# A hybrid encoder layer on one core: the mixer's gate branches as woven seven-product pairs, with the residual parked in DRAM

## The chip, the core and the metric

The kernel runs on one core of a Trainium2 chip. The core has five engines that work at the same time, each through its own instructions in order: TensorE (PE, matrix products), VectorE (DVE), ScalarE (ACT), GpSimd (POOL) and SyncE (SP), which here only issues transfers. On-chip data lie in SBUF, the results of matrix products in PSUM, here in eight banks of 128 x 512 float32. The metric is the device time of one execution in microseconds, lower being better; the median of several runs is given.

## The reference

One layer on 256 tokens with 2048 channels, all in float32:

```python
x = layer_norm(ALPHA*x + 0.5*swiglu(x, ffn1_w1, ffn1_w3, ffn1_w2), ln1_g, ln1_b)
mix = hybrid_mixer(x, w_in, ...)
x = layer_norm(ALPHA*x + mix, ln2_g, ln2_b)
x = layer_norm(ALPHA*x + 0.5*swiglu(x, ffn2_w1, ffn2_w3, ffn2_w2), ln3_g, ln3_b)
x = x + sigmoid(x @ w_ple_gate) * (p @ w_ple_proj)

# hybrid_mixer(x): IN_COLS = 13,320 columns of w_in
mq, mk, mv, mo, mi, mf, sq, sk, sv, ga, gb = split(x @ w_in)   # ga, gb: 2048 columns each
y_m  = mlstm(conv_silu(mq, mk), mv, mi, mf), normed per head, * sigmoid(mo)   # 4 heads of 256
y_sb = stick_breaking(sq, sk, sv)                                             # 8 heads of 128
merged = sigmoid(ga) * (y_m @ w_up_m) + sigmoid(gb) * (y_sb @ w_up_sb)
return merged @ w_out
```

The two FFNs have 5632 hidden channels. What matters here is `ga` and `gb`: both are products of the same x with two 2048 x 2048 blocks of `w_in`.

## The kernel before

Every product of activations and weights is made to float32 precision from three passes: the weight tile and the activation are each split into a high part (an ACT cast to float32r, L1066 for weights) and a low part (a DVE subtraction, L1070), and PE adds high x high, high x low and low x high (L1117 to L1119). A weight tile is 256 rows by 512 columns, 512 KB, loaded by SP (L1039) into a page called `raw`; its two halves of the split take two pages called `split`. The smallest piece of the program is a `Unit`: one weight tile against one half of the tokens (128 of 256), six matmuls. A plain `group` (L310) makes 512 columns from 8 weight tiles, 16 units in two PSUM banks, and each weight tile is split once for two units.

In the FFNs most pairs of up-projections (w1 and w3 on the same x) run as `seven` (L320): a scheme of Strassen's kind in Winograd's form. x, taken as 2 x 2 blocks (token halves by depth), times the two weight matrices side by side needs seven block products instead of eight. It needs sums of blocks. Sums of activations are made once per chunk (`form_turn`, L285, four DVE additions and two splits) into a second set of transposed activations, `act.forms`. Sums of weights are made in the raw page: an accumulating transfer on POOL's queue adds another quarter from DRAM into a page that has been split and used (`grow`, L334 to L337), or DVE adds two raw pages (`plus`, L339 to L344). The seven products are numbered and run in the order one, five, six, two, four and then seven and three in turn; each operand is split once for one unit. Four PSUM banks are in use in turn: X and E from the common pool, B and W the two fixed banks `seeded`. The order of several such pairs is chained (`chained`, L361), with empty places, and `weave` (L157) spreads this list evenly among the units of plain groups.

The whole order is written out ahead by a planner. It walks the list `program`, emits each unit, and keeps its own clock of PE time (L1120). Work that follows (transposes, heads, norm rows) is spawned with a delay on that clock from the table `DELAY` (L44) and emitted when due; `until` (L86) brings it forward where the next unit needs it. Splits are emitted as soon as fewer than SPLIT_MIX (6 in the mixer) tiles are split and unused, loads as soon as fewer than RAW_MIX (5 in the mixer) raw pages are held (L32, L33, L1020 to L1027, L1032). Each engine then executes its own instructions in exactly that order. SBUF holds 44 pages; PSUM has six banks in a common pool besides the two fixed ones.

The mixer before runs only plain groups, one after the other: the columns of q, the head gates, the other q and k, v, mo, the stick-breaking q, k and v, then the gate branches (`branch`, L908, ga and gb of a column group) and the up-projections (`ups`, L911), then w_out. Heads are spawned beside: `mlstm` (L761) and `stick` (L810), chains of small steps on PE, ACT, DVE and POOL (the masks at L834 and L842 are POOL's). The branches' results go through a sigmoid into pages `gt` (L885); `up_done` (L892) multiplies the up-projections into them. The residual `xres` (two tiles of 128 x 2048) stays in SBUF throughout: norm 1 writes it row by row (`rows`, L455, 16 DVE operations), and it is next read when w_out is added (`out_done`, L925).

Of the kernel before, what the change touches and what calls it, by code (L numbers as in the profile page):

```python
# [31 lines left out]
RAW_FFN, RAW_MIX, RAW_EDGE, RAW_HELD = 16, 5, 4, 8  # L32
SPLIT_FFN, SPLIT_MIX, SPLIT_EDGE, SPLIT_HELD = 5, 6, 11, 8  # L33
# [11 lines left out]
    "gb": 12.0, "form": 14.0, "ln_turn": 3.4, "ln_step": 1.2, "ln_low": 2.6, "h": 8.0, "silu": 6.0, "late": 9.0, "rest": 1.2, "mt": 3.2,  # L45
# [46 lines left out]
class ActT:  # L92


    def __init__(self, alloc, forms=None):
        self.alloc = alloc
# [84 lines left out]
def kernel(  # L181
# [16 lines left out]
    ps_pool = ctx.enter_context(tc.tile_pool(name="ps", bufs=PSUM_BUFS, space=bass.MemoryType.PSUM))  # L198
    seed_pool = ctx.enter_context(tc.tile_pool(name="seed", bufs=1, space=bass.MemoryType.PSUM))
# [12 lines left out]
    def drop(n=1):  # L212
        temps[0] -= n
# [66 lines left out]
    def finished(act, c, t):  # L280
        act.mark(c, t, 4)
        if act.forms and all(act.ready(c, h) for h in range(TT)):
            sched.spawn(form_turn(act, c), DELAY["form"] + 3.0 * c)
# [36 lines left out]
    def seven(wa, wb, rows, col0, cols, act, done):  # L320
# [24 lines left out]
        one, five, six, two, four, rest = [], [], [], [], [], []  # L345
        for i in range(n):
# [34 lines left out]
    class Norm:  # L381
        def __init__(self, g, b, act, alpha, delay, step):
            self.g_in, self.b_in, self.act = g, b, act
# [71 lines left out]
        def rows(self):  # L455
# [14 lines left out]
            pages[0] -= 4  # L470

# [106 lines left out]
    x1T = ActT(act_tile)  # L578
    norm1 = Norm(ln1_g[0], ln1_b[0], x1T, None, 30.0, 6.0)
# [4 lines left out]
    flags = set()  # L584

# [273 lines left out]

    head = group(w_in, range(0, D, 2 * P), 0, COL, x1T, qk_done(0, 0))  # L860
    program.extend(skewed(head[:SKEW]) + flat(head[SKEW:]))
    program.extend(flat(group(w_in, range(0, D, 2 * P), 4096, 2 * HM + 2 * DS, x1T, gates_done)))
    for which, g in ((0, 1), (1, 0), (1, 1)):
        program.extend(flat(group(w_in, range(0, D, 2 * P), which * 1024 + g * COL, COL, x1T, qk_done(which, g))))
    program.append(load_norm_m)
    program.append(lambda: [sched.spawn(in_sequence([mlstm(a), mlstm(a + 1)])) for a in (0, 2)])
    for g in range(2):
        program.extend(flat(group(w_in, range(0, D, 2 * P), 2048 + g * COL, COL, x1T, v_done(g))))
    for g in range(2):
        program.extend(flat(group(w_in, range(0, D, 2 * P), 3072 + g * COL, COL, x1T, mo_done(g))))  # L870
    first = 2
    for n in (4, 4, 4, 4, 4, 2):
        program.extend(flat(group(w_in, range(0, D, 2 * P), sq0 + first * DS, n * DS, x1T,
                                  lambda ps, t, f=first, n=n: sb_columns(ps, t, f, n))))
        first += n
        if first == 18:
            program.append(lambda: [sched.spawn(in_sequence([stick(a), stick(a + 2), stick(a + 4), stick(a + 6)]))
                                    for a in (0, 1)])
# [6 lines left out]
    def gate_done(g, half):  # L885
        def done(ps, t):
# [270 lines left out]
```

## Time and profile before

| | |
|---|---|
| median of 3 runs | 2210.81 us (2210.7 to 2211.28) |
| the profiled execution's own time | 2211.03 us, its span 2209.3 us |
| PE busy | 2194.2 us, 10068 matmuls |
| DVE busy | 1683.9 us |
| ACT busy | 1268.7 us |
| POOL busy | 187.5 us |
| splits of weight tiles on DVE | 1013, 1182.3 us |
| read from and written to DRAM | 497.96 MB, 2.10 MB |

The span runs from the first to the last instruction of the profiled execution. A row of a group names the line, the engine, the operation, the tiles written and read, their shapes and the count, then busy time and the mean of one in ns, then the idle time of the engine before it and what ended that. A row of waits gives the total, the number and the longest. In a row by stretch, each engine has its busy time and its instructions; then come the granted clock of PE, the share of the 16 transfer engines' time, and GB/s. Shares over 1 can occur, as transfers of several queues overlap.

### The profile page before, as it was taken

How to read it: one execution, taken by the hardware profiler on the slowest of the kernel's cores; microseconds unless marked ns; L12 is line 12 of the kernel's file. 1: busy time of each engine (PE TensorE's matmuls, PEld its weight loads, DVE VectorE, ACT ScalarE, POOL GpSimd, SP SyncE). 2: the span in 40 equal slices, each digit the busy share in tenths (PEclk: the TensorE clock that was granted, in tenths of full speed). 3: DMA queues.
4: the chain of work that ended last, by engine and by line, in shares of the span. 5: the costliest groups of instructions: out<-in, count | busy, mean ns of one | idle time of the engine just before them, and what ended most of it. 6: DMA issues, size and time to landing. Idle time of an engine off the chain costs nothing.

```text
span 2209.3 us, 27558 instructions
## 1 busy us (share of the span) xinstructions
PE 2194.2 (99%) x10068; PEld 1820.1 (82%) x10068; DVE 1683.9 (76%) x1859; ACT 1268.7 (57%) x1529; POOL 187.5 (8%) x167
## 2 busy tenths in 40 slices
PE   9999999999999999999999999999999999999999
PEld 7888888888887888888888888888888888888878
DVE  6889998888898784654445456599898989889884
ACT  6556566666575555545643344556666666666562
POOL 3111011110100000000100000011011111110000
PEclk9999999999999999999999999999999999999999
DMA  9899889987992765655566666579879998989643
GB/s 347 220 254 269 247 255 294 271 244 216 279 352 70 219 195 167 183 170 163 162 186 185 191 222 218 203 172 316 254 235 247 302 258 249 247 268 302 216 143 96
DMA packets 263050, 501.89 MB, mean 227 GB/s; under 512 B 15841, under 2 KB 24961, under 8 KB 262913
## 3 DMA queue, kind: packets, MB, share of 16 engines
q1 hardware_dynamic: 228096, 433.00, 59.0%
q0 software_dynamic: 34816, 67.12, 16.9%
q8 instruction: 79, 1.29, 0.2%
q14 instruction: 59, 0.48, 0.1%
HBM read 497.96 MB, written 2.10 MB: 226 GB/s over the span
## 4 chain that ended last, share of the span: by engine, by line
PE 96%; DMA 1%; DVE 1%; ACT 1%; issue 0%; DVEq 0%; ACTq 0%
PE mm L1119 27%; PE mm L1117 27%; PE mm L1118 27%; PE seeded L1117 4%; PE seeded L1119 4%; PE seeded L1118 4%; DMA raw<-in_ffn_w_dram 1%; PE ms L266 1%; DVE split L1070 1%; PE ms L436 0%; ACT split L1066 0%; PE ms L825 0%; PE ms L848 0%; PE ms L776 0%; PE ms L788 0%
## 5 line engine op out<-in xcount | busy, mean ns | idle before, releaser
L1070 DVE TENSOR_TENSOR split<-raw,split 128x1024 fp32r<-128x1024 f32 (+1 forms) x1013 | 1182.3, 1203 | 298.8 <-ACT split L1066 284.5
L1066 ACT CAST split<-raw 128x1024 fp32r<-128x1024 f32 (+1 forms) x1013 | 1018.2, 1037 | 458.0 <-PE mm L1118 123.8
L1117 PE MATMUL mm<-split,actT 128*128 128x512 f32 (+2 forms) x2768 | 1075.9, 389 | 3.1 <-ACT big L973 2.4
L1118 PE MATMUL mm<-split,actT 128*128 128x512 f32 (+2 forms) x2768 | 1064.4, 385 | 4.3 <-DVE split L1070 4.3
L1119 PE MATMUL mm<-split,actT 128*128 128x512 f32 (+2 forms) x2768 | 1065.0, 385 | 2.3 <-DVE actT L271 2.3
L1119 PEld LDWEIGHTS mm<-split,actT 128*128 128x128 f32 x2768 | 520.0, 188 | 107.3 <-DVE actT L271 3.1
L1118 PEld LDWEIGHTS mm<-split,actT 128*128 128x128 f32 x2768 | 520.5, 188 | 105.9 <-DVE split L1070 6.1
L1117 PEld LDWEIGHTS mm<-split,actT 128*128 128x128 f32 x2768 | 520.2, 188 | 104.9 <-ACT big L973 3.3
L336 POOL DMA_DIRECT2D raw<-in_ffn_w_dram x128 | 154.5, 1213 | 1303.5 <-DVE split L1070 646.3
L341 DVE TENSOR_TENSOR raw<-raw 128x1024 f32<-128x1024 f32 x128 | 155.8, 1217 | 11.0 <-DMA raw<-in_ffn_w_dram 11.0
L1117 PE MATMUL seeded<-split,actT 128*128 128x512 f32 x384 | 150.5, 392 | 0.0
L1119 PE MATMUL seeded<-split,actT 128*128 128x512 f32 x384 | 149.5, 389 | 0.0
L1118 PE MATMUL seeded<-split,actT 128*128 128x512 f32 x384 | 149.5, 389 | 0.0
L550 DVE SCALAR_TENSOR_TENSOR xres<-mm,xres 128x512 f32<-128x512 f32 x160 | 108.7, 684 | 22.0 <-PE mm L1119 22.0
L1119 PEld LDWEIGHTS seeded<-split,actT 128*128 128x128 f32 x384 | 72.1, 188 | 15.1
L1118 PEld LDWEIGHTS seeded<-split,actT 128*128 128x128 f32 x384 | 72.1, 188 | 14.7
L1117 PEld LDWEIGHTS seeded<-split,actT 128*128 128x128 f32 x384 | 72.1, 188 | 14.6
L268 ACT CAST actT<-ms 128x512 fp32r<-128x512 f32 x60 | 35.1, 587 | 67.2 <-PE ms L266 65.7
L271 DVE TENSOR_TENSOR actT<-ms,actT 128x512 fp32r<-128x512 f32 x60 | 41.0, 685 | 23.3 <-ACT actT L268 13.3
L238 ACT ACTIVATE temp<-mm 128x512 f32<-128x512 f32 (+1 forms) x38 | 21.8, 575 | 52.5 <-PE mm L1119 52.5
L238 ACT ACTIVATE big<-mm 128x512 f32<-128x512 f32 x20 | 12.0, 598 | 55.8 <-PE mm L1119 55.8
L234 ACT ACT_TABLE_LOAD x29 | 37.2, 1283 | 0.5
(137 smaller groups left out, 663.6 us busy)
## 6 DMA issues: line engine op xcount, KB each, us to landing
raw<-in_ffn_w_dram SPq DMA_DIRECT2D x527, 512.0 KB, 8.1
raw<-in_w_in_dram SPq DMA_DIRECT2D x168, 512.0 KB, 3.7
raw<-in_ffn_w_dram POOLq DMA_DIRECT2D x128, 512.0 KB, 9.5
raw<-in_w_out_dram SPq DMA_DIRECT2D x32, 512.0 KB, 4.7
raw<-in_w_ple_gate_dram SPq DMA_DIRECT2D x24, 512.0 KB, 4.8
raw<-in_w_up_m_dram SPq DMA_DIRECT2D x16, 512.0 KB, 3.9
raw<-in_w_up_sb_dram SPq DMA_DIRECT2D x16, 512.0 KB, 4.1
raw<-in_w_ple_gate_dram SPq DMA_DIRECT2D x16, 256.0 KB, 5.1
```

Of the source, the lines that this page charges most:

```text
L234: nc.scalar.preload_act_table_set(table[0])
L238: nc.scalar.activation(out, in_, func, **kw)
L268: nc.scalar.copy(dst[:, 0], ps[:])
L271: nc.vector.tensor_tensor(out=dst[:, 1], in0=ps[:], in1=dst[:, 0], op=ALU.subtract)
L336: nc.gpsimd.dma_start(out=raw.tile[:, :, :cols], in_=src.src, accum_op=ALU.add)
L341: nc.vector.tensor_tensor(out=a.tile[:, :, :cols], in0=a.tile[:, :, :cols], in1=b.tile[:, :, :cols], op=ALU.add)
L550: nc.vector.scalar_tensor_tensor(out=xs, in0=ps, scalar=0.5, in1=xs, op0=ALU.mult, op1=ALU.add)
L1066: nc.scalar.copy(hi[:, ks], r[:, ks])
L1070: nc.vector.tensor_tensor(out=lo[:, ks], in0=r[:, ks], in1=hi[:, ks], op=ALU.subtract)
L1117: nc.tensor.matmul(ps, hi, w[0][:, k, :u.cols], start=first, stop=False, skip_group_check=u.onto)
L1118: nc.tensor.matmul(ps, hi, w[1][:, k, :u.cols], start=False, stop=False, skip_group_check=u.onto)
L1119: nc.tensor.matmul(ps, lo, w[0][:, k, :u.cols], start=False, stop=last, skip_group_check=u.onto)
```

## The change

The gate branches become `gates7(g)`: for each of the four column groups, ga and gb are made as one seven-product pair from x1T and its sums. The pairs are chained and woven into all plain groups of the mixer from the k columns on, up to the up-projections of the first three groups. For that:

- x1T gets its second set with the sums of blocks (its delay is a new entry, 20).
- `seven` has a second form, `grown`: all sums of weights are made by accumulating transfers, none by DVE. Per depth it loads three quarters plainly and adds four; products three and seven use one buffer one after the other.
- Space: with x1T's sums kept through the mixer, the residual is copied to DRAM (`spill`, on POOL's queue) once norm 1's rows are done, and the gates of the first two column groups are kept in its place; it is read back (`refill`, eight transfers on SP's queue) before w_out. Norm 1's rows start and go faster (16 and 4 for 30 and 6).
- RAW_MIX goes from 5 to 8, SPLIT_MIX from 6 to 4.
- The heads run group by group: k and q of the first half, its v, its two mlstm heads, its mo, then the second half; the stick-breaking columns come in another order, so that the first four heads can start before the columns of the others. The up-projections of the first three groups run first with w_up_m, then with w_up_sb, and wait in the plan for the gates' flags.

```diff
-RAW_FFN, RAW_MIX, RAW_EDGE, RAW_HELD = 16, 5, 4, 8
-SPLIT_FFN, SPLIT_MIX, SPLIT_EDGE, SPLIT_HELD = 5, 6, 11, 8
+RAW_FFN, RAW_MIX, RAW_EDGE, RAW_HELD = 16, 8, 4, 8
+SPLIT_FFN, SPLIT_MIX, SPLIT_EDGE, SPLIT_HELD = 5, 4, 11, 8
...
-            two.append(unit(2, i, Weight(b21, [b21], []), act, 0, 2, "X", False))
-            four.append(unit(4, i, Weight(t, [], [t, b21], plus(t, b21)), act, 1, 2, "E", False))
             b12, b22 = quarter(wb, i, 0), quarter(wb, i, 2)
-            rest.append(unit(7, i, Weight(b12, [b12, b22], [b12], plus(b12, b22)), act.forms, 1, 0, "W", False))
-            rest.append(unit(3, i, Weight(b22, [], [b22]), act.forms, 1, 2, "B", False))
+            if grown:
+                w6.then = grow(t, quarter(wa, i, 2))
+                w2, w4 = Weight(b21, [b21], [b21]), Weight(t, [], [t])
+                w3, w7 = Weight(b22, [b22], []), Weight(b22, [], [b22])
+                w3.then = grow(b22, b12)
...
+        if grown:
+            rest = third[:1] + flat(zip(third[1:], seventh[:-1])) + seventh[-1:]
...
-    x1T = ActT(act_tile)
-    norm1 = Norm(ln1_g[0], ln1_b[0], x1T, None, 30.0, 6.0)
+    x1T = ActT(act_tile, ActT(act_tile), "form1")
+    norm1 = Norm(ln1_g[0], ln1_b[0], x1T, None, 16.0, 4.0, lambda: sched.spawn(spill(), 6.0))
...
+    def spill():
+        for t in range(TT):
+            nc.gpsimd.dma_start(out=kept[t][:], in_=xres[t][:])
+        flags.add("spilt")
...
+    def refill():
+        for c in range(4):
+            for t in range(TT):
+                cs = slice(c * COL, (c + 1) * COL)
+                nc.sync.dma_start(out=xres[t][:, cs], in_=kept[t][:, cs])
+        flags.add("refilled")
...
+    main = columns(1024, COL, qk_done(1, 0))
     for g in range(2):
+        if g:
+            main += columns(COL, COL, qk_done(0, 1)) + columns(1024 + COL, COL, qk_done(1, 1))
+        else:
+            main.append(load_norm_m)
+        main += columns(2048 + g * COL, COL, v_done(g))
+        main.append(lambda g=g: sched.spawn(in_sequence([mlstm(2 * g), mlstm(2 * g + 1)])))
+        main += columns(3072 + g * COL, COL, mo_done(g))
+    for first, n in ((2, 4), (8, 4), (16, 4), (6, 2), (12, 4), (20, 4)):
+        main += columns(sq0 + first * DS, n * DS, lambda ps, t, f=first, n=n: sb_columns(ps, t, f, n))
+        if first == 16:
+            main.append(lambda: [sched.spawn(in_sequence([stick(a), stick(a + 2), stick(a + 4), stick(a + 6)]))
+                                 for a in (0, 1)])
...
+    def gates7(g):
+        def done(m, banks):
+            ps = {k: v["ps"][:] for k, v in banks.items() if v}
+            if m == 5:
+                for t in range(TT):
+                    gt[g, t] = xres[t][:, g * 1024:(g + 1) * 1024] if g < 2 else big()[:]
+                e = temp()
+                nc.scalar.copy(e[:], ps["E"])
+                banks["B"]["ps"], banks["W"]["ps"] = seeded
+                nc.vector.tensor_tensor(out=banks["B"]["ps"][:], in0=ps["X"], in1=e[:], op=ALU.subtract)
+                drop()
+            elif m == 6:
+                nc.scalar.copy(banks["W"]["ps"][:], ps["B"])
+            elif m == 4:
+                nc.scalar.copy(gt[g, 1][:, 0:COL], ps["E"])
+            elif m == 2:
+                sched.spawn(gate(0, 0, ps["X"], 1.0), DELAY["silu"])
+            elif m == 7:
+                c = gt[g, 1][:, 0:COL]
+                nc.vector.tensor_tensor(out=c, in0=ps["W"], in1=c, op=ALU.add)
+                sched.spawn(gate(1, 1, ps["W"], -1.0))
+                sched.spawn(gate(1, 0, c, 1.0), DELAY["silu"])
+            elif m == 3:
+                sched.spawn(gate(0, 1, ps["B"], -1.0))
...
     def up_done(g, half):
         def done(ps, t):
+            sched.until(lambda: ("gate", g, half, t) in flags)
...
-    program.extend(branch(0, 0) + branch(0, 1) + branch(1, 0) + branch(1, 1))
-    program.extend(ups(0) + ups(1))
-    program.extend(branch(2, 0) + branch(2, 1) + ups(2))
-    program.extend(branch(3, 0) + branch(3, 1))
+    for half in range(2):
+        for g in range(3):
+            main += ups(g, half)
+    program.extend(weave(main, chained([gates7(g) for g in range(4)])))
     program.append(lambda: [sched.spawn(merge_turn(g, t), 1.0 + 2.0 * g + t) for g in range(3) for t in range(TT)])
-    program.extend(ups(3))
+    program.append(lambda: sched.spawn(refill(), 14.0))
+    program.extend(ups(3, 0) + ups(3, 1))
```

More of the change, by code (lines that the diff above doesn't have):

```diff
@@ L343, in plus @@
             return make
-        one, five, six, two, four, rest = [], [], [], [], [], []
+        one, five, six, two, four, seventh, third = [], [], [], [], [], [], []
         for i in range(n):
@@ L470, in rows @@
             pages[0] -= 4
+            if self.then:
+                self.then()
     def scaled(xs):
@@ L584 @@
     flags = set()
+    kept = [dram_pool.tile([P, D], F32, name=f"kept{t}") for t in range(TT)]
+    def spill():
+        for t in range(TT):
+            nc.gpsimd.dma_start(out=kept[t][:], in_=xres[t][:])
+        flags.add("spilt")
+        return
+        yield
+    def refill():
[4 more added lines that the diff above has]
+        flags.add("refilled")
+        return
+        yield
     def mixer_setup():
```

66 lines of the change are left out of this document (32 added, 34 removed).

## The prediction

> **What bounds the kernel now.** I read the page's head and its chain of waits first. Its totals by engine, then its chain by engine:
>
> ```profile
> span 2209.3 us, 27558 instructions
> ...
> PE 2194.2 (99%) x10068; PEld 1820.1 (82%) x10068; DVE 1683.9 (76%) x1859; ACT 1268.7 (57%) x1529; POOL 187.5 (8%) x167
> ...
> PE 96%; DMA 1%; DVE 1%; ACT 1%; issue 0%; DVEq 0%; ACTq 0%
> ```
>
> PE is busy for 99% of the span and carries 96% of the chain that ends last, so a matmul taken out is worth its whole time, provided nothing else becomes late. Next, what PE waited for between 690 and 1430 us, which is the mixer with the two norms beside it:
>
> ```profile
> engine line waited for: us in total, times, longest us
> PE mm L1118 <- DVE split L1070: 2.2, 2, 1.1
> ```
>
> Two waits, 2.2 us in all: in the whole mixer PE hardly stops. Third, busy time by stretch: the woven first FFN (100 to 540), two stretches of the mixer's plain groups, and two short stretches where transfers come thickest.
>
> ```profile
> core 0: us, PE busy (x) PEld busy (x) DVE busy (x) ACT busy (x) POOL busy (x), PEclk, DMA share, GB/s
> 100.00:540.00 440.00, 440.00 (x1973) 364.44 (x1972) 389.85 (x384) 271.94 (x290) 57.80 (x48) 1.00 0.90 257
> 730.00:830.00 100.00, 100.00 (x501) 84.33 (x500) 81.16 (x116) 57.43 (x80) 0.00 (x0) 1.00 0.68 205
> 830.00:1000.00 170.00, 170.00 (x774) 139.67 (x773) 92.30 (x142) 84.89 (x110) 8.14 (x8) 1.00 0.58 168
> ...
> 720.00:730.00 10.00, 10.00 (x55) 8.64 (x54) 3.44 (x6) 2.83 (x7) 0.00 (x0) 1.00 0.91 299
> ...
> 1430.00:1440.00 10.00, 10.00 (x45) 8.27 (x45) 6.84 (x10) 5.61 (x8) 0.00 (x0) 1.00 1.04 384
> ```
>
> The FFN already weaves seven-product pairs into plain groups: DVE 389.85 of 440 us (89%), DMA share 0.90, and PE still 440.00 of 440. The mixer has room: DVE 54% to 81%, DMA 0.58 to 0.68. The granted clock is 1.00 throughout.
>
> **The products removed.** The pace of PE, from the first and last matmul of an undisturbed stretch in order of time:
>
> ```profile
> 1139.71 0.39 PE L1119 MATMUL mm<-split,actT 128*128 128x512 f32 x1
> ...
> 1149.91 0.39 PE L1119 MATMUL mm<-split,actT 128*128 128x512 f32 x1
> ```
>
> These are 46 matmuls, so 45 steps in 10.20 us: 0.2267 us each (the 0.39 us shown is a pipelined duration). A unit of the program is six matmuls, 1.360 us. The branches of one column group are now 2 x 8 weight tiles x 2 token halves = 32 units; as a seven-product pair they are 4 depths x 7 = 28. Over four groups 16 units go, 96 matmuls: 96 x 0.2267 = 21.8 us. Everything else on PE (groups, transposes, heads) keeps its count; it is only ordered anew.
>
> **What it adds off PE.** The groups of instructions, different shapes apart:
>
> ```profile
> L1070 DVE TENSOR_TENSOR split<-raw,split 128x1024 fp32r<-128x1024 f32 x979 | 1159.7, 1220 | 282.0 <-ACT split L1066 267.8 <-PE mm L1118 6.0 <-DMA raw<-in_w_in_dram 1.9
> ...
> L1066 ACT CAST split<-raw 128x1024 fp32r<-128x1024 f32 x979 | 999.1, 1052 | 451.2 <-PE mm L1118 123.8 <-PE mm L1119 92.2 <-DVE split L1070 70.6
> ...
> L336 POOL DMA_DIRECT2D raw<-in_ffn_w_dram x128 | 154.5, 1213 | 1303.5 <-DVE split L1070 646.3 <-DMA raw<-in_ffn_w_dram 636.6 <-DVE xres L550 20.0
> ...
> L234 ACT ACT_TABLE_LOAD x29 | 37.2, 1283 | 0.5
> ...
> L504 DVE TENSOR_TENSOR seeded<-mm,temp 128x512 f32<-128x512 f32 x16 | 11.1, 696 | 5.9 <-ACT temp L510 5.9
> ...
> L510 ACT COPY temp<-mm 128x512 f32<-128x512 f32 x16 | 9.4, 585 | 14.2 <-PE mm L1119 14.2
> ...
> L291 DVE TENSOR_TENSOR temp<-temp,big 128x256 f32<-128x256 f32 x8 | 3.7, 462 | 0.3
> ```
>
> A plain weight tile is split once for two units, a seven-product operand once for one: 112 splits where 64 were, 48 more. DVE gets 48 x 1.220 = 58.6 us, the sums of four chunks of x1T at most 4 x (4 x 0.462 + 2 x 0.696) = 13.0, and two ops of 0.69 a group, 5.5: together 77 us. ACT gets 48 x 1.052 = 50.5, eight casts and twelve copies of about 0.6, 12, and up to 24 table loads (each sigmoid batch between exponentials, 31 us): 62 to 93. The woven stretch is 352 full units and 16 of 256 columns (half as many columns, so some 0.7 us, an estimate from the pace above), 352 x 1.360 + 11 = 490 us. There two splits, one plain and one of the pairs, stand in about 4.08 us: 2.44 us of DVE, 60%. The heads' own DVE work is what the 830 stretch holds beside its splits, which alone are:
>
> ```profile
> 830.00:1000.00 170.00, 158.73 (x670) 124.15 (x669) 65.67 (x56) 55.14 (x56) 1.00 0.58 168
> ```
>
> 92.30 - 65.67 = 26.6 us in 170 (third column), 16%. So 76%, below the FFN's 89% at which PE loses nothing: cost 0, hidden under PE. Were that cover gone, the 77 us would count from DVE's first full stretch.
>
> The earlier norm rows (delay 16 for 30) and the sums of x1T fall in the first 60 us of the mixer, where DVE has 81% and gets some 12 us more. That is about full for a while. The lead of the splits absorbs it; I take 0, at most 4.
>
> **Transfers.** FFN first, then the mixer: queues (packets, MB, share of 16 engines), and issues with the median time to landing.
>
> ```profile
> q1 hardware_dynamic: 45477, 87.65, 57.8%
> q0 software_dynamic: 13056, 25.17, 31.7%
> ...
> raw<-in_ffn_w_dram SPq DMA_DIRECT2D x166, 512.0 KB, 7.8
> raw<-in_ffn_w_dram POOLq DMA_DIRECT2D x48, 512.0 KB, 9.5
> ```
>
> ```profile
> q1 hardware_dynamic: 15340, 28.50, 57.5%
> ...
> raw<-in_w_in_dram SPq DMA_DIRECT2D x51, 512.0 KB, 3.6
> ```
>
> The change drops 16 of 64 plain loads of gate weights and adds 64 accumulating ones on POOL's queue, 2.1 MB of the residual out (POOL's queue) and 2.1 MB back (SP's). A plain load takes all 16 engines for 0.578 x 440 / 167 = 1.52 us in the FFN and 0.575 x 170 / 54.4 = 1.80 us in the thin traffic of the mixer; in the thick traffic of the 720 row 9.1 us / 2.99 MB x 0.524 MB = 1.60. An accumulating load takes 0.317 x 440 / 48 = 2.9 us. In the weave: 144 plain loads of w_in, 8 halves, 24 of the up weights, 64 accumulating, and the spill (4 loads' worth). With 1.60 that is 148 x 1.60 + 28 x 1.52 + 64 x 2.9 = 465 us in 490, share 0.95; with 1.52 it is 0.92; with 1.80 and the accumulating loads dearer in the same ratio (3.4) it is 527, more than the stretch. I take 0.95: a little above the FFN's 0.90, and the 1430 row shows that 1.04 and 384 GB/s can be carried.
>
> Is each load early enough? RAW_MIX is 8, but a pair holds up to four first quarters, and in the third/seventh phase (seven side places of 4.08 us, 28 us a group) two sums besides: only 2 to 3 buffers are left for loads, and a load is wanted every 2.8 us (172 loads in 490 us). Sustained, 2.5 buffers allow 2.5 x 2.8 = 7 us from issue to split. A landing of L makes the splits late by 28 x (1 - 7/L) a group, less the lead of the splits (SPLIT_MIX 4: four units stand between, 5.5 us). At the FFN's L = 7.8: 2.9 us, covered. At 10: 8.4 - 5.5 = 2.9 us on PE, 12 over four groups. So 0 to 12; I take 1, since 7.8 is the row with the nearest load.
>
> The accumulated operands:
>
> ```profile
> DMA to landing us min/median/max: 5.9/9.5/14.3
> ```
>
> The shortest gap from a split to the next use of the same buffer is third to seventh: two side places, 8.2 us, plus 5.5 of lead, 13.6 us, at five places (last group's first and last, the others' last with 15.0). Wanted: 2.3 (split) + 9.5 + 2.3 = 14.1. So 0 to 0.5 us each at the median, 5 each at the longest landing: 0 to 25, I take 1.
>
> **Heads, queues, residual.** POOL works in order, and the selects of the heads now stand behind accumulating issues of 1.2 us that wait for their split; who waits for the selects is PE. The selects' own view, then POOL in order of time, then two of PE's steps in the chain:
>
> ```profile
> L834 POOL TENSOR_SCALAR_AFFINE_SELECT temp<-temp x8: 589/729/1389, 1015.4 to 1093.3; 128x256 f32<-128x256 f32 x8
> ```
>
> ```profile
> 1043.27 1.95 POOL L834 TENSOR_SCALAR_AFFINE_SELECT temp<-temp 128x256 f32<-128x256 f32 x2 [17.49 <-DVE temp L833]
> ```
>
> ```profile
> 1047.87 0.65 PE ms L838 x2
> ...
> 1074.05 0.65 PE ms L838 x2
> ```
>
> Between the selects' end (1045.22) and PE's step lie 2.65 us. One issue with its 1.2 us fits; an issue whose split is queued (2.3 us more) makes 0.9 late. Eight such steps: 0 to 7. X and E hold two of six PSUM banks and the main group two, so each pair of stick heads has just two; 12 double steps at one 0.59 us copy: 0 to 7. The last heads start when sv's second half is there (395 us into the weave by the order's unit times) and at 1074.05 - 1047.87 = 26.2 us a pair end just when ups want them (449): 0 to 5. I take 1 for all. The new wait of the up-projections for the gates is on a flag of the plan, and the sigmoids lie many units ahead of it.
>
> The spill is issued some 60 us (by the unit times) before the first gate value is written over the residual, and 2.1 MB at the rates above are 6 us; ACT, with the splits queued behind that gate, would wait only beyond that. The refill is put in SP's queue behind loads and waits for the last transposes of groups 0 and 1; behind it stand the w_out loads. It is issued 7 us before the last up-projections end, and the residual is first read 16 units, 22 us, after that; 6 us of transfer are covered by the eight buffers, which hold only main weights by then. Cost 0; without that cover, 6.
>
> Sum: profiled execution 2211.0 us (span 2209.3 and 1.7 around it, 0.2 above the median of 2210.81): 2211.0 - 21.8 + 1 + 1 + 1 = 2192.
>
> **The rivals.** (1) Short buffers: landings near 10 us, +12 in place of +1: 2203. For: the low-buffer phase and 27% of accumulating transfers, against the FFN's 22%. Against: landings are 3.6 us now, and few requests in flight queue less. (2) Heads late under the weave: selects behind issues and PSUM banks short, +14 in place of +1: 2205. For: POOL has one order, DVE is fuller. Against: heads run in one stream a group now, and a select's longest is 1.39 us. [...]
>
> (3) Transfers of w_in are dearer than I take: halfway from 1.60 to 1.80, with accumulating loads in the same ratio (2.9 x 1.70 / 1.52 = 3.24): 148 x 1.70 + 43 + 64 x 3.24 = 502, 12 over the stretch, 2211.0 - 21.8 + 12 + 2 = 2203. For: 1.80 in the mixer. Against: 1.60 where traffic is thick, as it will be. [...]
>
> (4) The other side: transfers bound the weave. Price: 527 us in 490, +37, so 2211.0 - 21.8 + 37 = 2226. It turns the sign once they pass 490 + 21.8 = 512. For: 1.80, and an accumulating load of w_in has no row, so 3.4 is open. Against: 1.80 with today's accumulate price is only 148 x 1.80 + 43 + 186 = 495, and 1.80 is measured where few loads overlap.
>
> **How the numbers follow.** Forecast 60% (2189 to 2197), (1) 13%, (2) 9%, (3) 8%, (4) 10%. The measurement tells about 0.2%, 4.4 us, from no change: faster is below 2206.4, slower above 2215.2. Forecast and most of (1), (2) and (3) are faster: 83%. Their tails and the start of (4) are the same: 6%. The rest is slower: 11%. The range goes from 2188 (no loss at all is 2189.2) to 2209, past (1) to (3), and leaves out (4).
>
> **What would show it.** PE 96 matmuls fewer (9972) and busy 22 us less; L1070 x1061; POOL's issues of in_w_in x64, landing near 9 us; DMA share about 0.95 in the weave, against 0.58 to 0.68; PE's waits in the mixer below 6 us. Wrong if PE waits for splits whose cast waited for raw transfers (1, 3, 4), or for selects, copies or PSUM (2), or if DVE is at 100% through the weave.

## The result, and the profile after

The changed kernel takes 2228.65 us (median of four runs, 2227.91 to 2231.02), the kernel before beside it 2211.05: a ratio of 1.0081, with an interval of 1.0063 to 1.0098. It is 17.6 us slower, where 18.8 us faster was forecast and the range ended at 2209.

The page's head, three groups and two rows of transfers of the kernel after. A group's row has busy time and mean of one in ns, then idle time before it; a transfer's row has count, size and median time to landing:

```profile
span 2226.7 us, 27777 instructions
...
PE 2187.3 (98%) x9972; PEld 1804.9 (81%) x9972; DVE 1755.1 (79%) x1935; ACT 1332.3 (60%) x1600; POOL 265.5 (12%) x233
...
L1133 DVE TENSOR_TENSOR split<-raw,split 128x1024 fp32r<-128x1024 f32 (+2 forms) x1061 | 1242.4, 1206 | 276.5 <-ACT split L1129 258.9
L1129 ACT CAST split<-raw 128x1024 fp32r<-128x1024 f32 (+2 forms) x1061 | 1065.1, 1038 | 454.2 <-PE mm L1181 112.1
...
L337 POOL DMA_DIRECT2D raw<-in_w_in_dram x64 | 77.2, 1207 | 453.4 <-DVE split L1133 388.2
...
raw<-in_w_in_dram SPq DMA_DIRECT2D x152, 512.0 KB, 4.9
...
raw<-in_w_in_dram POOLq DMA_DIRECT2D x64, 512.0 KB, 7.9
```

The counts are those worked out: 9972 matmuls, 96 fewer; 1061 splits, 48 more; 64 accumulating loads. The other work is near its estimate too: DVE has 71.2 us more (77 were estimated), ACT 63.6 (62 to 93). In this listing the cast of a split is L1129, its subtraction L1133, and the three matmuls are L1180 to L1182. Without 21.8 us of matmuls the span would be 2187.5, so 39.2 us are lost somewhere.

What PE waited for between 690 and 1440 us (total, times, longest):

```profile
PE mm L1181 <- DVE split L1133: 15.9, 17, 2.3
PE mm L1180 <- ACT split L1129: 3.9, 5, 1.4
PE ms L798 <- DVE actT L262: 3.0, 2, 1.8
PE mm L1180 <- DVE big L677: 1.1, 1, 1.1
PE seeded L1180 <- ACT split L1129: 1.0, 1, 1.0
PE seeded L1181 <- DVE split L1133: 0.8, 1, 0.8
PE ms L881 <- DVE actT L262: 0.7, 1, 0.7
PE ms L746 <- ACT temp L734: 0.3, 2, 0.2
```

Where the kernel before had two waits of 2.2 us in all, these are thirty waits of 26.7 us, most of them for a split (L1133 and L1129). Each is short. By stretch (columns: length; busy time of PE, PE's weight loads, DVE, ACT, POOL; granted clock, share of the transfer engines, GB/s), first before, then after:

```profile
730.00:790.00 60.00, 60.00 (x319) 51.18 (x318) 49.36 (x71) 36.56 (x52) 0.00 (x0) 1.00 0.70 209
790.00:1350.00 560.00, 560.00 (x2580) 464.46 (x2579) 306.09 (x385) 280.40 (x363) 18.66 (x24) 1.00 0.61 183
```

```profile
730.00:790.00 60.00, 50.80 (x248) 40.36 (x247) 51.30 (x84) 30.86 (x47) 4.85 (x4) 0.94 0.65 169
790.00:1350.00 560.00, 544.38 (x2478) 445.28 (x2477) 364.83 (x438) 341.30 (x432) 91.90 (x86) 1.00 0.88 234
```

PE is idle for 9.2 us in the first 60 us of the weave and for 15.6 in the rest. DVE is busy for 365 of the 560 us, 65%, and the transfers for 0.88: neither is full on average. Everything ahead of the mixer and behind norm 2 takes as long as before: norm 1's transposes start at 694.5 us (694.1 before), and from norm 2's first transpose to the end of the span it is 809.4 us (809.6 before).

Two places of the kernel after, in order of time (start, duration, instruction, in brackets the idle time before it and what ended it). ACT, then DVE, when the head gates are made:

```profile
745.65 1.04 ACT L1129 CAST split<-raw 128x1024 fp32r<-128x1024 f32 x1
754.59 0.42 ACT L239 ACTIVATE big<-big 4x256 f32<-4x256 f32 x1 [7.90 <-DVE big L704]
755.03 1.28 ACT L235 ACT_TABLE_LOAD   x1
...
757.18 1.98 ACT L1129 CAST split<-raw 128x1024 fp32r<-128x1024 f32 x2
```

```profile
748.41 0.69 DVE L475 TENSOR_TENSOR xres<-xres,big 128x512 f32<-128x512 f32 x1
749.14 0.69 DVE L476 TENSOR_TENSOR xres<-xres,big 128x512 f32<-128x512 f32 x1
749.75 1.29 DVE L262 TENSOR_TENSOR actT<-temp,actT 128x512 fp32r<-128x512 f32 x2
750.95 0.42 DVE L291 TENSOR_TENSOR temp<-big 128x256 f32<-128x256 f32 x1
...
752.42 1.22 DVE L1133 TENSOR_TENSOR split<-raw,split 128x1024 fp32r<-128x1024 f32 x1
...
754.10 0.46 DVE L704 TENSOR_SCALAR big<-ms,bf 4x256 f32<-4x256 f32 x1
758.24 1.23 DVE L1133 TENSOR_TENSOR split<-raw,split 128x1024 fp32r<-128x1024 f32 x1 [3.69 <-ACT split L1129]
```

ACT's next instruction in order is a step of the head gates that needs DVE's L704. DVE comes to it only after norm rows (L475, L476), low parts and sums of x1T (L262, L291 to L294) and a split. ACT stands still for 7.9 us with the casts of the next splits behind that step, and from the end of one cast to the start of the next (746.69 to 757.18) 10.5 us pass; then DVE stands still for 3.7 us, because no cast is ready; then PE waits. The same happens in each convolution, where ACT's scaling of the second half waits for DVE's three additions on the first:

```profile
933.95 0.48 ACT L239 ACTIVATE temp<-ms,cw 128x256 f32<-128x256 f32 x1
936.77 0.47 ACT L239 ACTIVATE temp<-ms,cw 128x256 f32<-128x256 f32 x1 [2.35 <-DVE temp L757]
```

And a wait of PE can have a tail. PE in order of time after its longest wait at the start:

```profile
746.28 0.50 PE L1181 MATMUL mm<-split,actT 128*128 128x512 f32 x1 [2.28 <-DVE split L1133]
746.62 0.39 PE L1182 MATMUL mm<-split,actT 128*128 128x512 f32 x1
...
747.40 0.63 PE L1182 MATMUL mm<-split,actT 128*128 128x512 f32 x1
747.83 0.63 PE L1180 MATMUL mm<-split,actT 128*128 128x512 f32 x1
...
749.97 0.63 PE L1182 MATMUL mm<-split,actT 128*128 128x512 f32 x1
```

One microsecond after the wait, seven matmuls start 0.43 us apart ((749.97 - 747.40) / 6) in place of 0.227, and the granted clock is 0.50 from 747.4 to 750.2 us and 0.94 over the stretch from 730 to 790. There are three such spells in the mixer, 21 matmuls, 4.3 us beyond the waits; most of the thirty waits have none behind them.

So of 39.2 us, 24.5 are new visible waits (26.7 - 2.2) and 4.3 slow matmuls; some 10 are in no row. Part of these are restarts: where no second wait follows, the matmul behind one that waited mostly starts 0.31 to 0.34 us after it (746.28 to 746.62 above) in place of 0.227, for thirty waits some 3 us (an estimate from those rows, 30 x 0.11). By place the visible waits (27.0 us, with a few too short for the rows above) are 9.2 us at the start (730 to 790), 4.9 at the convolutions, 5.1 at the mlstm heads and where a head's step waits for a PSUM bank, 3.8 at the stick-breaking rounds, 1.8 at the last pair's accumulated operand, and 2.2 at the two norms as before.

### The profile page after: what moved, and what is told of

It is laid out like the page before. It is cut to its first block, busy times and chain, and to the rows that moved or that the text cites. A ratio compares the mean times of both kernels' runs of the same rounds, so it can differ in the third digit from the quotient of the medians.

```text
span 2226.7 us, 27777 instructions
## 1 busy us (share of the span) xinstructions
PE 2187.3 (98%) x9972; PEld 1804.9 (81%) x9972; DVE 1755.1 (79%) x1935; ACT 1332.3 (60%) x1600; POOL 265.5 (12%) x233
## 4 chain that ended last, share of the span: by engine, by line
PE 45%; issue 2%; ACT 1%; DMA 1%; DVE 1%; ACTq 0%; POOLq 0%; POOL 0%; DVEq 0%
PE mm L1181 12%; PE mm L1180 12%; PE mm L1182 12%; PE seeded L1181 2%; PE seeded L1182 2%; PE seeded L1180 2%; DMA raw<-in_w_in_dram 1%; PE ms L267 1%; ACT split L1129 0%; ACT temp L239 0%; DVE split L1133 0%; PE ms L449 0%; PE ms L871 0%; PE ms L881 0%; ACT big L1036 0%
## 5 line engine op out<-in xcount | busy, mean ns | idle before, releaser
L1133 DVE TENSOR_TENSOR split<-raw,split 128x1024 fp32r<-128x1024 f32 (+2 forms) x1061 | 1242.4, 1206 | 276.5 <-ACT split L1129 258.9
L1129 ACT CAST split<-raw 128x1024 fp32r<-128x1024 f32 (+2 forms) x1061 | 1065.1, 1038 | 454.2 <-PE mm L1181 112.1
L1181 PE MATMUL mm<-split,actT 128*128 128x512 f32 (+2 forms) x2640 | 1018.0, 386 | 17.8 <-DVE split L1133 17.8
L1180 PE MATMUL mm<-split,actT 128*128 128x512 f32 (+2 forms) x2640 | 1027.7, 389 | 7.7 <-ACT split L1129 4.1
L1182 PE MATMUL mm<-split,actT 128*128 128x512 f32 (+2 forms) x2640 | 1016.7, 385 | 2.3 <-DVE actT L272 2.3
L1181 PEld LDWEIGHTS mm<-split,actT 128*128 128x128 f32 x2640 | 497.3, 188 | 120.0 <-DVE split L1133 25.0
L1180 PEld LDWEIGHTS mm<-split,actT 128*128 128x128 f32 x2640 | 497.1, 188 | 107.4 <-ACT split L1129 8.0
L1182 PEld LDWEIGHTS mm<-split,actT 128*128 128x128 f32 x2640 | 496.8, 188 | 102.1 <-DVE actT L272 3.1
L1180 PE MATMUL seeded<-split,actT 128*128 128x512 f32 x480 | 189.0, 394 | 1.0 <-ACT split L1129 1.0
L1181 PE MATMUL seeded<-split,actT 128*128 128x512 f32 x480 | 187.8, 391 | 0.9 <-DVE split L1133 0.8
L1182 PE MATMUL seeded<-split,actT 128*128 128x512 f32 x480 | 187.5, 391 | 0.0
L337 POOL DMA_DIRECT2D raw<-in_w_in_dram x64 | 77.2, 1207 | 453.4 <-DVE split L1133 388.2
L1181 PEld LDWEIGHTS seeded<-split,actT 128*128 128x128 f32 x480 | 90.4, 188 | 20.3 <-DVE split L1133 2.1
L1180 PEld LDWEIGHTS seeded<-split,actT 128*128 128x128 f32 x480 | 90.3, 188 | 19.9 <-ACT split L1129 1.8
L1182 PEld LDWEIGHTS seeded<-split,actT 128*128 128x128 f32 x480 | 90.4, 188 | 18.9
L239 ACT ACTIVATE temp<-mm 128x512 f32<-128x512 f32 (+1 forms) x38 | 21.8, 575 | 63.7 <-PE mm L1182 63.6
```

Of the source, the lines that this page charges most:

```text
L337: nc.gpsimd.dma_start(out=raw.tile[:, :, :cols], in_=src.src, accum_op=ALU.add)
L1129: nc.scalar.copy(hi[:, ks], r[:, ks])
L1133: nc.vector.tensor_tensor(out=lo[:, ks], in0=r[:, ks], in1=hi[:, ks], op=ALU.subtract)
L1180: nc.tensor.matmul(ps, hi, w[0][:, k, :u.cols], start=first, stop=False, skip_group_check=u.onto)
L1181: nc.tensor.matmul(ps, hi, w[1][:, k, :u.cols], start=False, stop=False, skip_group_check=u.onto)
L1182: nc.tensor.matmul(ps, lo, w[0][:, k, :u.cols], start=False, stop=last, skip_group_check=u.onto)
```

## The theories

**A.** What PE has in hand is the lead of the splits: with n tiles held, n - 1 stand ahead of PE. A plain tile lasts two units, an operand of a pair one; in the weave that is 1.5 units of 1.360 us on average. Before: 5 x 2 x 1.360 = 13.6 us. After, with four: 3 x 1.5 x 1.360 = 6.1 us. ACT and DVE work in order, and the heads, the norm rows and the sums come in bursts in which ACT makes no cast for more than 6 us, at the longest, in the weave, for the 10.5 us above. The old lead covered them, the new one doesn't. Two parts are told apart: **A1**, the work on DVE at the start, and **A2**, ACT standing still in its order for a result of DVE. **B**: the accumulating transfers and the raw buffers are what is late (the prediction's own rivals 1, 3 and 4).

## The experiments

### Transfers or lead

e1: an accumulating load brings only half its bytes.

```diff
-                nc.gpsimd.dma_start(out=raw.tile[:, :, :cols], in_=src.src, accum_op=ALU.add)
+                ks = slice(0, 1 if grown else 2)
+                nc.gpsimd.dma_start(out=raw.tile[:, ks, :cols], in_=src.src[:, ks], accum_op=ALU.add)
```

> Each accumulating transfer of the gate pairs adds only the first of its two 128-row halves, so half the bytes on POOL's queue in the mixer; the second half of the weight sums is left out of the result. Theory A (splits too few ahead, so that bursts of other work on ACT and DVE reach PE): transfers are not what is late, only the last pair's waits for accumulated operands go, 2224 to 2229 us. Rival B (transfers bound the weave, the fourth rival of the prediction): 64 x 1.45 = 93 us of transfers less in the weave, so most of the 39 us lost comes back, 2190 to 2200 us.

Measured: 2224.02 us, ratio 1.0058 (1.0043 to 1.0073). The stretch from 790 to 1350:

```profile
790.00:1350.00 560.00, 546.83 (x2497) 448.88 (x2496) 365.07 (x438) 344.98 (x434) 71.34 (x86) 1.00 0.75 208
```

The transfer share falls from 0.88 to 0.75 and PE gains 2.5 us in 560. What ACT's casts waited for transfers between 725 and 1420, in the changed kernel and then in e1:

```profile
ACT split L1129 <- DMA raw<-in_w_in_dram: 41.6, 14, 7.4
ACT split L1130 <- DMA raw<-in_w_in_dram: 11.1, 9, 4.1
```

Casts that wait for raw transfers are the sign that the prediction named for its rivals 1, 3 and 4, and the changed kernel has them. With e1 three quarters of these waits go, yet PE's waits for splits only fall from 21.6 to 19.4 us. Half the accumulated bytes are worth 4.6 us at most; B isn't the main cause.

e2: one split less, SPLIT_MIX 3 for 4. e4: the kernel before with SPLIT_MIX 3 for 6, a lead of 2 x 2 x 1.360 = 5.4 us, and nothing else.

> The changed kernel with SPLIT_MIX 3 for 4, all else equal. Theory A: one split less ahead of PE (about 4.1 us of lead for 5.5), PE's waits in the mixer rise from 26 us to 40 or more, 2240 to 2260 us. Rival B: the transfers are the same, 2226 to 2231 us.

> The kernel before with SPLIT_MIX 3 for 6 and nothing else: two other weights of two units each stand between a split and its use, 5.4 us of lead, as in the changed kernel, but no pairs, no accumulating transfers, DMA share unchanged near 0.6. Theory A: PE's waits of 10 us or more appear in the mixer at the same kinds of bursts (convolutions, head norms, stick heads), 2220 to 2235 us. Rival B: no change, 2210 to 2212 us.

Measured: e2 2262.9 us, 1.0233 (1.0216 to 1.025); e4 2223.64 us, 1.0056 (1.0041 to 1.0071). PE's waits in the mixer, e2:

```profile
PE mm L1181 <- DVE split L1133: 23.1, 25, 2.1
PE mm L1180 <- ACT split L1129: 12.3, 9, 2.8
```

and e4:

```profile
PE mm L1118 <- DVE split L1070: 7.5, 8, 1.8
PE mm L1117 <- ACT split L1066: 1.8, 3, 1.4
```

e4 is the clearest row of the study. There is no pair, no accumulating load and no sum in that mixer, its transfer share is 0.59 (690 to 1440), and a lead of 5.4 us, a little shorter than the changed kernel's 6.1, costs 12.6 us by itself. e2's time lies 3 us above what was expected; its direction and its waits are A's.

e3: one split more (5), paid with a raw page (RAW_MIX 7), since the pages are all in use.

> The changed kernel with SPLIT_MIX 5 for 4 and RAW_MIX 7 for 8 (a raw page given up for the two split pages, since the pages are full). Theory A: lead 6.8 us for 5.5, PE's waits in the mixer fall by about a third, 2216 to 2224 us. Rival B: one load less in flight in a stretch bound by transfers, 2229 to 2240 us.

Measured: 2229.53 us, 1.008 (1.0065 to 1.0095). The waits for splits fell from 21.6 to 13.7 us, but waits for steps of the heads rose, ACT's waits for transfers went from 41.6 us in 14 to 52.6 in 24, and nothing was gained. Whether the page or the longer lead did that, this run doesn't tell.

### Taking the bursts away

e6 (A2): ACT isn't made to wait in its order. Both scalings of a convolution come ahead of DVE's additions, and the plan lets splits in between a DVE result and the ACT step that reads it.

```diff
                 activate(acc[:, k], ps[:, k], ACT.Copy, scale=w(3))
+            for k in range(2):
+                ...
                 for j in range(3):
...
+        yield 4.0
         activate(sp, zf, ACT.Abs)
...
+        yield 1.3
         activate(st["em"][:], ps[:, 1], ACT.Exp, scale=-1.0)
...
+            yield DELAY["m2"]
             activate(hs[:, t], ps[:, 0:DM], ACT.Copy, scale=r[:, t:t + 1])
```

> The changed kernel with the small steps of the heads put in another order, the work the same: in the convolution both ACT scalings before the DVE additions; one planner step between DVE's result and the ACT step that wants it in the head gates and in mlstm. ACT then waits less for DVE with splits queued behind it. Theory A2 (ACT blocked in order, with 5.5 us of lead): the gaps at the convolutions and mlstm steps (about 6 us with 2 to 4 of tail) go, 2217 to 2224 us. Rival (only the number of splits ahead matters, blocks move elsewhere): 2226 to 2231.

Measured: 2213.78 us, 1.0014 (1.0005 to 1.0023): 14.9 us less than the changed kernel, from the order of a few ACT steps, and more than was expected. ACT's waits for the DVE results concerned (head gates, convolutions, mlstm) fall from 59.6 to 24.2 us. PE's visible waits fall by 6.5 us (26.7 to 20.2), its slow matmuls from 21 to 14; the rest of the gain is in no row. e12, the same edit in the kernel before:

> Control: the kernel before with the same reordering of the heads' small steps and nothing else. Its splits lead PE by about 14 us, so ACT's waits behind DVE are covered: 2210 to 2212 us. If the reordering saves time by itself, below 2208.

2211.71 us, 1.0002 (0.9992 to 1.0011). With a lead of 13.6 us the same ACT stalls cost nothing.

e5 (A1): norm 1's rows move from DVE to POOL, which is busy for 4.85 of the 60 us there.

```diff
-                        nc.vector.tensor_tensor(out=xs, in0=xs, in1=g, op=ALU.mult)
-                        nc.vector.tensor_tensor(out=xs, in0=xs, in1=b, op=ALU.add)
+                        eng = nc.gpsimd if self.then else nc.vector
+                        eng.tensor_tensor(out=xs, in0=xs, in1=g, op=ALU.mult)
+                        eng.tensor_tensor(out=xs, in0=xs, in1=b, op=ALU.add)
```

> The changed kernel with the 16 operations of norm 1's rows on POOL instead of DVE (11 us less on DVE in the first 60 us of the mixer). Theory A1 (part of the loss is DVE being full at the mixer's start, 730 to 790 us: 9 us of PE's 27 us of gaps and two of its three slow spells): about half of these 9 us and of their tail go, 2217 to 2224 us. Rival (the start does not matter, the bursts later do): 2226 to 2231.

Measured: 2239.05 us, 1.0125 (1.011 to 1.0141), 10 us more. From 730 to 790, a group of DVE in the changed kernel and the same in e5, a group of POOL in e5, and e5's whole stretch:

```profile
L262 DVE TENSOR_TENSOR actT<-temp,actT 128x512 fp32r<-128x512 f32 x8 | 5.1, 682 | 0.0
L262 DVE TENSOR_TENSOR actT<-temp,actT 128x512 fp32r<-128x512 f32 x8 | 10.4, 1340 | 0.0
```

```profile
L477 POOL TENSOR_TENSOR xres<-xres,big 128x512 f32<-128x512 f32 x6 | 11.2, 1872 | 0.5
```

```profile
730.00:790.00 60.00, 43.64 (x203) 34.17 (x202) 53.26 (x65) 27.31 (x41) 25.61 (x16) 0.86 0.58 143
```

DVE did 65 instructions in 53.26 us where it did 84 in 51.30. Some of the other work on DVE took longer: L262 1340 ns a piece for 682, L293 692 for 418. Two pairs of L262 in e5, the first beside two of POOL's rows (747.04 to 750.63), the second after POOL's last (782.58):

```profile
746.79 4.38 DVE L262 TENSOR_TENSOR actT<-temp,actT 128x512 fp32r<-128x512 f32 x2
785.05 1.28 DVE L262 TENSOR_TENSOR actT<-temp,actT 128x512 fp32r<-128x512 f32 x2
```

A third pair, at 776.99, took 1.27 us, and POOL's operation beside it (775.73) took 4.01 us, where POOL's other eleven took 1.32 to 2.27. In these two places one engine or the other took longer; by what means, no run shows. That the accumulating loads, which POOL also issues in order, came later behind the rows may have its part; no run separates the two. e8, e5 and e6 together with the second stream of stick heads 7 us later:

> The changed kernel with the rows on POOL, the unblocked order of the heads' steps, and the second stream of stick heads 7 planner us after the first, so that eight ACT steps in one burst become four and four. Theory A: the three causes add, 2206 to 2216 us. Rival B: 2222 to 2231.

2225.26 us, 1.0068 (1.0053 to 1.0083). That is 11.5 us more than e6: with the rows on POOL most of e6's gain is gone.

e7: where splits and a head's step are due at once, the splits are emitted first.

```diff
+        if [m for e, m in edges if e <= pos["split"]][-1:] == [True]:
+            splits_due()
         sched.run()
```

> The changed kernel with one line in the planner's loop, in the mixer alone: splits that have become due are emitted before the due steps of the heads instead of after them. Nothing is added or removed. Theory A: a split no longer queues behind the burst emitted at the same moment, PE's waits for splits (20 us) fall by a third or more, 2210 to 2222 us. Rival B (transfers): 2226 to 2231.

2227.87 us, 1.0078 (1.0061 to 1.0095): no gain. The splits' waits fell to 16.4 us, and the head steps, now later, made PE wait themselves (2.9 us for a convolution's copy, 3.9 for a PSUM bank). Changing places doesn't shorten a burst.

### Spacing the rest

Three kernels with e6's edit. e9: the weave begins 8 places later and the rows later and slower (24 and 5 for 16 and 4). e10: without that; the last pair's sevenths come one place later, and the next mlstm head and the convolution's first step 1.4 us later. e11: both, and the second stick stream 7 us later.

```diff
-    program.extend(weave(main, chained([gates7(g) for g in range(4)])))
+    program.extend(weave(main, [None] * 8 + chained([gates7(g) for g in range(4)])))
...
-    ... "cv0": 1.0,
+    ... "cv0": 2.4,
...
         drop()
+        yield 1.4
...
+            if last:
+                rest = third[:3] + [seventh[0], third[3]] + seventh[1:]
```

> The kernel of the unblocked order (2213.8 us) with the weave begun eight side places (some 22 us) later and norm 1's rows at delay 24 and step 5 for 16 and 4. Theory A1 (what is left at the mixer's start, 5 us of gaps and a slow spell of PE between 733 and 795 us, is DVE carrying rows, sums, head gates and the pairs' splits at once): 2205 to 2210 us. Rival (the same work is late wherever it stands, and the weave becomes denser behind): 2212 to 2218.

> The kernel of the unblocked order with three waits taken away by distance: in the last pair the seventh products stand one place further behind the third ones, the next mlstm head and the convolutions' first step start 1.4 planner us later. Theory (PSUM banks and the last accumulated operands make PE wait 2.9 + 1.2 + 2.3 us with one slow spell): 2206 to 2211 us. Rival (their waits only uncover the next ones): 2212 to 2215.

> Both together, with the second stream of stick heads 7 planner us after the first. If the causes add, the gaps left are the two at the norms and a few near 1 us, and the 21.8 us of removed products appear: 2193 to 2203 us. If the short lead of the splits finds new bursts: 2203 to 2212.

Measured: e9 2214.34 us, 1.0012 (1.0003 to 1.0021), nothing against e6, so A1's forecast for it missed. e10 2209.22 us, 0.9991 (0.9982 to 1.0001). e11 2206.39 us, 0.9978 (0.9969 to 0.9987): the whole computation, 4.8 us faster than the kernel before and 22.3 faster than the changed one. Its stretches:

```profile
730.00:790.00 60.00, 55.73 (x289) 46.18 (x288) 56.34 (x94) 41.32 (x61) 4.82 (x4) 0.97 0.69 185
790.00:1350.00 560.00, 554.24 (x2539) 455.57 (x2538) 370.06 (x440) 343.89 (x432) 92.13 (x86) 1.00 0.89 241
```

After 790 us 9.9 of the 15.6 us of idle time are gone, at the same transfer share; at the start 4.3 remain, 3.05 of them in one wait.

### A longer lead with no page given up, and the start

e13 to e15 let x1T's two sets of sums share pages, which frees four; the second set is written over the first, so that part of the gates' products uses the wrong sums. e13 leaves them empty, e14 makes two more splits of them (SPLIT_MIX 6, a lead of 5 x 1.5 x 1.360 = 10.2 us), e15 does the same to e11.

```diff
-            self.tiles[c, tt] = self.alloc()
+            self.tiles[c, tt] = self.get(c, 0) if self.one and tt else self.alloc()
...
+    x1T.forms.one = True
```

> Control for the next run. The two sets of sums of x1T share one set of pages (the second is written over the first, so that products five and six multiply the sums meant for seven and three: this part of the gates' computation is changed, the amount of work is not). Four pages stand empty, all else is the changed kernel. Every theory: as the changed kernel, 2224 to 2231 us, 30 to 40 visible waits of PE in the mixer, 23 to 30 us.

> As the control, with the four pages given to two more pairs of split pages: SPLIT_MIX 6, RAW_MIX still 8 (the gates' computation is changed in the same part). Theory A (the lead of the splits, some 5.5 us with four, is shorter than the bursts; with six it is some 8 to 9 us): most bursts of 5 to 8 us are covered again, visible waits fall from some 27 us to 5 to 13, time 2194 to 2210 us. Rival C (the engines' full stretches, not the lead, set the waits: a longer lead only moves them): waits stay above 18 us, time 2217 to 2231.

> The reordered and spaced kernel (all_spaced) with shared sums and SPLIT_MIX 6 (the gates' computation is changed as in the two runs before). Theory A: both remedies act on the same waits, what is left of them nearly goes: waits 0 to 6 us, time 2190 to 2199 us, the predicted 2192 in reach. Rival C: as all_spaced, 2202 to 2208.

Measured: e13 2231.54 us, 1.0092 (1.0077 to 1.0107); e14 2222.77 us, 1.0055 (1.0038 to 1.0072); e15 2209.0 us, 0.9991 (0.9981 to 1.0). Stretches and first waits of e14:

```profile
730.00:790.00 60.00, 45.43 (x229) 36.74 (x226) 48.57 (x78) 29.31 (x44) 4.82 (x4) 0.93 0.65 173
790.00:1350.00 560.00, 552.58 (x2525) 455.91 (x2526) 369.36 (x443) 346.69 (x439) 92.61 (x86) 0.99 0.89 237
```

```profile
PE ms L747 <- ACT temp L735: 7.5, 3, 7.1
PE mm L1182 <- DVE split L1134: 7.1, 6, 2.3
PE mm L1181 <- ACT split L1130: 3.2, 1, 3.2
```

Neither theory came out whole. e13 is 2.9 us above the changed kernel, so e14's gain from the lead is 8.8 us against e13; its time lies in rival C's range. After 790 us the longer lead does what A says: idle time falls from 14.2 us in e13 (545.85 busy) to 7.4. At the start it makes things worse, 14.6 us idle for 11.6 (48.43 busy): a convolution's transposes waited 7.1 us for a copy on ACT. More lead means more splits ahead of each head step in the same two queues; that this moves the wait from the splits to the heads is likely, but not shown. On top of e11 it gains nothing, so A's expectation of e15 was wrong too.

e16 to e18 leave norm 1's 16 row operations out on DVE: in e14, in e11 and in the changed kernel.

```diff
-                    if self.alpha is None:
+                    if self.then:
+                        pass
+                    elif self.alpha is None:
```

> As e14 (shared sums, SPLIT_MIX 6), and norm 1's rows are left out on DVE: the 16 multiplications and additions of the gain and the bias on the residual aren't made, so the residual lacks them (and the gates' sums are shared as in e14). Theory S (DVE's queue at the start, where rows, sums of x1T and head gates stand ahead of the splits, makes the waits from 730 to 790 us): these fall from 15 us to below 6, time 2204 to 2213 us. Rival T (they come from ACT's waits for other steps, or from the transfers at the weave's start, and the rows only fill idle time): they stay above 11 us, time 2219 to 2224.

> As e11 (everything reordered and spaced, SPLIT_MIX 4, pages and sums as in the changed kernel), with norm 1's rows left out on DVE as in e16. Theory S: the remaining wait of 3 us near 768 us and the spell of slow matmuls behind it go, time 2198 to 2203 us. Rival T: as e11, 2204 to 2208.

> The changed kernel with norm 1's rows left out on DVE as in e16 and nothing else. Theory S: the waits from 730 to 790 us fall from 9 us to below 4 and their slow spells go, time 2216 to 2222 us. Rival T: 2226 to 2231.

Measured: e16 2214.67 us, 1.0016 (1.0006 to 1.0025), 8.1 less than e14; e17 2199.89 us, 0.995 (0.9934 to 0.9967), 6.5 less than e11; e18 2222.28 us, 1.0049 (1.0034 to 1.0064), 6.4 less than the changed kernel. Stretches of e17:

```profile
730.00:790.00 60.00, 59.08 (x308) 49.53 (x307) 54.27 (x88) 43.71 (x61) 4.82 (x4) 1.00 0.73 207
790.00:1350.00 560.00, 554.41 (x2542) 456.39 (x2541) 361.03 (x428) 342.72 (x430) 92.20 (x86) 1.00 0.89 241
```

The rows are worth 6.4 to 8.1 us in three kernels, and in e17 the start's wait and its slow spell are gone (59.08 of 60 at a clock of 1.00). In e16 and e18 the start keeps some idle time beside, for 52.07 and 54.25 us of 60 are busy; ACT's stalls, which e6 removes, are still in these two. The sizes were forecast a little too large for e16 and e18.

Over all the runs A's times came out in e1, e4, e10, e12 and e17, lay somewhat outside in e2, e6, e13, e16 and e18, and missed in seven: e3, e7, e8, e9 and e14 fell in the rival's range, e5 and e15 above both. So the runs bear A out on what the waits are, and much less on what a given remedy brings.

## Why the prediction was wrong, point by point

- **The matmuls removed: right.** 9972 matmuls, splits and issues to the count. PE's busy time fell by only 6.9 us (2194.2 to 2187.3), since slow matmuls count as busy (4.3 us), and so does the first matmul after a wait, shown with 0.50 us for 0.39; the rest of the difference is in no row. With most of the waits taken away, e17 stands 11.4 us below the kernel before; it leaves out no work of PE, but the 16 row operations on DVE.
- **"76%, below the FFN's 89% at which PE loses nothing: cost 0, hidden under PE": the step that failed.** The work was sized rightly, and the share was even lower, 65%. But a share says whether the work fits, not whether it comes in time. What had to be set against each other are the longest stretch in which ACT makes no cast (10.5 us from 746.69, 7.9 of them idle) and the lead (6.1 us). In the FFN, which has no heads beside it, ACT goes 4.4 us at most without a cast (100 to 540), against four tiles ahead (five are held there) at one cast every 1.83 us (440 / 240), 7.3 us; it was the wrong row to compare with. The prediction counted SPLIT_MIX's lead, 5.5 us by its own reckoning, and held it in numbers only against late loads and accumulated operands. e4 shows the price of such a lead alone, 12.6 us; e6 with e12 shows that of ACT's stalls, 14.9 us with the short lead and nothing with the long one.
- **"The lead of the splits absorbs it; I take 0, at most 4": wrong on the same ground.** The start loses 9.2 us of visible waits, and leaving the rows out gives 6.4 back (e18).
- **Heads, "I take 1 for all": too small.** PSUM banks alone are 3.7 us of waits (L798 and L881), and spacing steps of heads and the last pair's sevenths gave 4.6 (e10 against e6). Rival 2 priced this at 14; the short PSUM banks that it named are there, the selects on POOL, its other half, stand in no row of PE's waits.
- **Transfers: nearly right.** The share was 0.88 for 0.95, an accumulating load landed in 7.9 us for 9.5. Short buffers and accumulated operands, 1 us each, cost up to 4.6 together (e1). A plain load cost what the forecast took, 1.60 us: SP's queue (q1) moved 97.24 MB from 790 to 1350 us in 52.8% of the 16 engines' time, 0.528 x 560 / 97.24 x 0.524 = 1.59 us a load.
- **Rival 4 gave nearly the right time, 2226, by luck.** It asked for 527 us of transfers in 490. The share shows 0.88, and halving the accumulated bytes left 13.0 of the 17.6 us.
- **Residual: right at 0.** No wait of PE in the mixer stands at the copy out or the way back.

The loss is 39.5 us by the medians (2228.65 less the 2189.2 of no loss at all). By the runs in order: ACT's stalls 14.9 (e6), spacing 4.6 (e10) and 2.8 (e11), leaving the rows out 6.5 (e17). That leaves 10.7 us; 6.3 are visible waits (8.5 us in e17's rows, less the 2.2 of before); slow spells are gone, and some 4 us are in no row. The steps were made in one order, so a share could stand under a neighbour. Open is also why more lead hurts at the start: the place was seen, moving it was not tried.

## What to carry to other kernels

Before hiding work under a busy engine by its mean share, work out the lead that the feeding engines have (buffers held, less the one in use, times what each lasts) and compare it with their longest stretch without feeding, as a timeline shows it. A lead that is short isn't the whole of it: here a longer one made the start worse. An edit that halves how long each buffer lasts halves the lead, whatever the shares say. When that is short, first look for an in-order engine that waits for another engine's result with feeding work queued behind: putting that step later cost nothing here and gave more (14.9 us) than two more buffers did (8.8, e14 against e13).

## What the runs showed of the hardware

- **A wait of PE can be paid twice.** After 2.28 us of idle time seven matmuls ran at 0.43 us for 0.227, at a granted clock of 0.50. In e2 such spells came to 66 matmuls, some 13.4 us (66 x 0.203) beside 44.8 us of waits; in e17, whose waits are all of 1.13 us or less, there were none. The mean granted clock of the profiled execution was 0.991 in e2, 0.997 in the changed kernel and 1.00 in e17.
- **POOL was no free engine for elementwise work beside DVE (e5).** With 12 operations of 1.8 us on POOL, each 0.69 us on DVE, DVE's L262 took twice as long in the same stretch (1340 ns for 682).
- **An accumulating load landed in 7.9 us where a plain one took 4.9**, the same 512 KB, under a transfer share of 0.88; with half the bytes it landed in 4.7. The one goes by POOL's queue, the other by SP's; no run separates the queue from the addition.
